# Shifted operand addresses and an earlier place for one triangular inverse in a two-layer hybrid backbone kernel

## The chip, the cores and the metric

The kernel runs on one core of a Trainium2 chip. The metric is the device time of one execution in microseconds; lower is better. The kernel before takes 1970.32 us, the median of three runs from 1968.26 to 1972.65. The computation is in float32 throughout; where a dense product is meant, each operand is split into a high and a low part and three products (high x high, high x low, low x high) are summed.

## The reference, cut to what matters

Two layers act on 512 latent tokens and 256 context tokens of width 1024. Every sub-layer is an RMS norm, a modulation by vectors from the conditioning (adaLN), the work itself, another RMS norm, a gate and a residual sum.

```
layer 0: mixer = [spatial-gating MLP | bidirectional RWKV-7, 8 heads] behind one input projection (2944 columns),
         then one output product; then ConvFFN on latents and context
layer 1: mixer = bidirectional mLSTM, 4 heads, behind one input projection; output product;
         then ConvFFN on latents only

def conv_ffn(h, w_up, conv_w, conv_b, w_down, rows):
    a, b = jnp.split(h @ w_up, 2, axis=-1)          # w_up: 1024 x 5632
    a = dwconv1d(a, conv_w[1]) if rows is None else dwconv_grid(a, conv_w, rows)
    return (jax.nn.gelu(a + conv_b) * b) @ w_down   # w_down: 2816 x 1024

def rwkv7_scan(...):                                # one step per token, per head, per direction
    sa = einsum('bhvk,bhk->bhv', s, kk_t)
    s = s * w_t - sa[..., None] * b_t + v_t[..., None] * k_t
    y_t = einsum('bhvk,bhk->bhv', s, r_t)
```

The kernel does the RWKV scan in chunks of 64 tokens. Inside a chunk the steps depend on one another through a lower triangular matrix with ones on its diagonal, which has to be inverted for each chunk, head and direction.

## The kernel before, in words

**Dense products.** Weights are streamed from HBM by `load_w` (L118): a raw tile of 1024 columns, its high part written by ACT (L124) and its low part by DVE or POOL (L125). `proj_pass` (L259 to 269) multiplies one such tile, 8 blocks of 128 columns as weights in PE, by the 8 blocks of the transposed activations as the moving operand, 512 columns for the latents and 256 for the context: a pass is 24 matmuls into one PSUM bank, L266, L267 and L268 in turn. `down` (L1033) has it the other way: the activations' blocks are the weights in PE, and half of the streamed weight tile, 512 columns, is the moving operand, L1043 to L1045, with two PSUM banks per token tile. `proj_pass` serves layer 0's input projection, layer 1's and both FFNs' first products; `down` serves both output products and both FFNs' second products.

**Where tiles lie.** All on-chip tiles come from pools that are stacked in each partition's memory, some from the left end and some (`side="right"`) from the right. A tile's bytes are rounded up to a multiple of 32. What was allocated before decides a tile's address. In the built program the operands of dense products begin at these places beyond a multiple of 512 bytes: the projection of layer 0 has activations and weights at 480; the later stages have weight tiles at 352, normalized activations at 480, and the FFN's hidden activations (`hhi`, `hlo`) at 224. The last of these lie behind the tile `fpar`, which holds the FFN's convolution parameters, 220 columns.

**Layer 0's mixer** has two stages. In the projection stage the 8 heads are prepared as four pairs ("column tiles" `ct` 0 to 3): projections with a short convolution (`kr`, `v`), decay and key terms (`prep_e`), the chunks' triangular matrices (`prep_n`) and their inverse (`prep_t`, L580). Finished sets are stored to HBM. In the chain stage they are loaded back, and a recurrence walks over the chunks of two pairs at a time, one `lane` each, first pairs 0 and 1, then 2 and 3, in six blocks.

`prep_t` copies the matrix's diagonal blocks through a DVE transpose (L585), sets an identity on POOL (L587, L588), and then does 31 substitution steps, two DVE instructions each (L597, L599). It then transposes the result, copies it into the tile `TT` on ACT (L613, L614), makes the off-diagonal blocks by two rounds of small matmuls (L621, L630) with copies between (L624, L633), and stores `TT` to HBM (L636). All its work tiles have one buffer, which the next pair's inverse needs again.

**What sets the order.** The pieces are Python generators. `weave` takes from several of them in turn, by the share of each one's steps that has been emitted (a third number delays a generator's start). Each `prep_t` yields after every third substitution step, after the copies to `TT`, and four times in the matmuls: 15 times in all. The framework then plans each engine's queue: emission order is the priority, and a planner with modelled durations gives an engine that would be idle the next instruction that is ready, even if it was emitted later. On the chip every queue runs in that planned order. The inverses of the third and the fourth pair (`ct` 2 and 3) are `Ts[0]` and `Ts[1]`; they are emitted in blocks 0 and 1 of the chain stage. `inverse()` runs `Ts[1]` and then frees the inverses' memory, in which the loads for the next modulation vectors (`ada_job`) are placed.

Of the kernel before, what the change touches and what calls it, by code (L numbers as in the profile page):

```python
# [8 lines left out]
F32 = mybir.dt.float32  # L9
# [5 lines left out]
P = 128  # L15
# [36 lines left out]
PF = _Cols()  # L52
# [22 lines left out]
def _build(ctx, tc, xall, par, cst, ada_0, ada_w, ada_t, w_in, w_out, ffn_up, ffn_down, lora, wsT, a_bs, c_in, c_gate, c_out, mneg, parf, parm, out):  # L75
# [9 lines left out]
    def bank(name, role):  # L85

        turn[role] = turn.get(role, -1) + 1
        return pp.tile([P, 512], F32, tag=role[turn[role] % len(role)], name=name)
# [201 lines left out]
    def woven(*gens):  # L290

        live = [[g[0], 0, g[1], g[2] if len(g) > 2 else 0.0] for g in gens]
        while live:
            k = min(range(len(live)), key=lambda j: live[j][3] + (1 - live[j][3]) * (live[j][1] + 0.5) / live[j][2])
            try:
                next(live[k][0])
                live[k][1] += 1
            except StopIteration:
                live.pop(k)
            yield  # L300

    def weave(*gens):
        for _ in woven(*gens):
            pass

    def part_of(g, n):
        for _ in range(n):
            next(g)
            yield

    def run(gen):
        for _ in gen:
            pass
# [16 lines left out]
    with ExitStack() as lx:  # L330
# [102 lines left out]
        prbank = lambda name: bank(name, "2435")  # L433
# [119 lines left out]
        def prep_n(ct):  # L553

            s = st[ct]
            RBv = s["RB"].rearrange("p (u a t) -> p u a t", a=2, t=64)
            LBv = s["LB"].rearrange("p (u a t) -> p u a t", a=2, t=64)
            NF = wkT.tile([P, 56, 32], F32, tag="NF", name=f"NF{ct}", bufs=2)
            G.memset(NF[:, 24:32], 0.0)
            G.memset(NF[:, 32:56], 0.0)  # L560
            for g8 in range(3):
                px, py = bank(f"nx{ct}{g8}", "23"), bank(f"ny{ct}{g8}", "45")
                for k in range(8):
                    u = g8 * 8 + k
                    mm(px[0:64, k * 64:k * 64 + 64], LBv[0:64, u, u // 12, :], RBv[0:64, u, 0, :], start=True, stop=True)
                    mm(py[64:128, k * 64:k * 64 + 64], LBv[64:128, u, u // 12, :], RBv[64:128, u, 0, :], start=True, stop=True)
                us = slice(g8 * 8, g8 * 8 + 8)
                for (pp, b0, e) in ((px, 0, A), (py, 64, A)):
                    p3 = pp.rearrange("p (u t) -> p u t", t=64)
                    cpy = e.copy if e is A else e.tensor_copy  # L570
                    off = slice(32 + g8 * 8, 40 + g8 * 8)
                    cpy(NF[b0:b0 + 32, us], p3[b0:b0 + 32, :, 0:32])
                    cpy(NF[b0 + 32:b0 + 64, us], p3[b0 + 32:b0 + 64, :, 32:64])
                    cpy(NF[b0 + 32:b0 + 64, off], p3[b0:b0 + 32, :, 32:64])
                yield
            for k in ("RB", "LB"):
                nc.sync.dma_start(set_part(ct, k), s[k])
            s["NF"] = NF
# [270 lines left out]
        def kr(ct):  # L849
            st[ct] = {}  # L850
            for c0, tag in ((12, "kT"), (8, "rT")):
                st[ct][tag] = conv_tile(c0 + ct, wkP, tag, f"{tag}{ct}", 2)
                yield
# [5 lines left out]
        def chained(*gens):  # L859
            for g in gens:  # L860
                yield from g

        def start_prep(ct):
            PLt = keep.tile([P, 24], F32, name=f"PL{ct}")
            st[ct]["PL"] = PLt
            for k, n in SET:
                if k not in ("vT", "TT"):
                    st[ct][k] = wkS.tile([P, n], F32, tag=k, name=f"{k}{ct}")
            return prep_e(ct, st[ct]["kT"], st[ct]["rT"])
# [13 lines left out]
                yield  # L883

        NA = (4, 6, 6)
        run(kr(0))
        weave((start_prep(0), 8), (chained(v(0), kr(1), part(0)), 3 + 0))
        run(prep_n(0))
        for ct in range(3):
            n = NA[ct]  # L890
            weave(*([(prep_t(ct, prbank), 13, 0.0)] if ct < 2 else []), (chained(start_prep(ct + 1), prep_n(ct + 1)), 9 + 3, 0.0),
                  (chained(v(ct + 1), *([kr(ct + 2)] if ct < 2 else []), part(n)), 3 + n, 0.0))
        run(SG)
        ex.close()
        hx.close()
        rx.close()
        sx.close()
        Ts = [prep_t(ct, lambda name: bank(name, "7")) for ct in (2, 3)]
        fin = lx.enter_context(tc.tile_pool(name="fin0", bufs=1))
        ch = lx.enter_context(tc.tile_pool(name="chain0", bufs=1))  # L900
        ys = [[fin.tile([P, 2, w], F32, name=f"y{n}{w}") for w in (TC, TL)] for n in ("01", "23")]
# [50 lines left out]
        def inverse():  # L952
            yield from Ts[1]
            tx.close()
            late["p"] = lx.enter_context(tc.tile_pool(name="late0", bufs=1))
            nc.scalar.dma_start(lwg, lora[:, 1024:1536])
# [16 lines left out]
        for b, (k, g) in enumerate(blocks):  # L973
            n = (22, 20, 22 - 10 * k)[g]
            todo = [(part_of(C[k], n) if g < 2 or k else C[k], n)]
            if b < 5:
                kk_, gg_ = blocks[b + 1]
                todo.append((preps(pairs[kk_], gg_), 10))
            if b == 0:
                todo.append((Ts[0], 13))  # L980
            elif b == 1:
                todo.append((inverse(), 13))
            elif b < 5:
                todo.append((part_of(ada, (5, 6, 5)[b - 2]), (5, 6, 5)[b - 2]))
            if b == 3:
                for ct in range(2):
                    load_bv(ct)
                todo.append((finish((0, 1), ys[0], ("01", "01"), "ctx"), 8))
            elif b == 4:
                todo.append((finish((0, 1), ys[0], ("01", "01"), "lat"), 8))  # L990
            elif b == 5:
                todo.append((finish((2, 3), ys[1], ("01", "01"), "ctx"), 8))
            weave(*todo)
            if g < 2:
                run(part_of(C[k], 4))
            if b == 1:
                ada = ada_job([1, 2], late["p"], 2, 2048)
            if b == 2:
                C.append(chains(pairs[1], ys[1]))
            if b == 4:  # L1000
                run(ada)
                gate_rows(0, 0, "7")
                scale_vec(0, 1)
                load_bv(2)
                load_bv(3)
# [53 lines left out]
    def ffn(l, xt, hT, ctx_too, after, final=None, beneath=None):  # L1059

        with ExitStack() as fx:
            hidp = fx.enter_context(tc.tile_pool(name=f"fhid{l}", bufs=1))
            hid = [hidp.tile([P, NH, w], F32, tag=f"hid{g}", name=f"hid{l}{g}") for g, w in ((0, TL), (1, TC))[:2 if ctx_too else 1]]
            fpar = hidp.tile([P, PF.n], F32, name=f"fpar{l}")
            nc.scalar.dma_start(fpar, parf[l])
            sp = fx.enter_context(tc.tile_pool(name=f"fs{l}", bufs=1))
            fill = beneath(sp) if beneath else None
# [71 lines left out]


    strm.sub, strm.hi, strm.lo = nc.vector, 3, 3
    xp = ctx.enter_context(tc.tile_pool(name="x", bufs=1))
    H = {tg: ctx.enter_context(tc.tile_pool(name=f"H{tg}", bufs=1, side="right")) for tg in ("lat", "ctx")}
    xcx = ExitStack()
# [464 lines left out]
```

## Time and profile before

| what | value |
|---|---|
| median of three runs | 1970.32 us (1968.26 to 1972.65) |
| the profiled execution: device time, span | 1975.72 us, 1973.8 us |
| PE busy, DVE busy | 1854.0 us (94%), 1334.4 us (68%) |
| ACT busy, POOL busy | 800.1 us (41%), 306.9 us (16%) |
| granted PE clock, mean | 0.965 |
| HBM read, written | 199.31 MB, 26.39 MB |

The stages lie in the span about so: projection stage up to 377 us, chain stage to 625, output product to 700, FFN of layer 0 to 1270, mixer of layer 1 to 1540, output product to 1590, FFN of layer 1 to the end. Matmuls are pipelined: a matmul's own duration in the profile is longer than the time after which the next one starts, so the pace of a stream of them is read from their starts, or from their count in a stretch of time. Times in a single row are microseconds from the span's start, and line numbers are those of the kernel before.

### The profile page before, as it was taken

What the parts mean: (1) busy time and instruction counts of PE and PEld (TensorE: products, weight loads), DVE (VectorE), ACT (ScalarE), POOL (GpSimd) and SP (SyncE); (2) the same over time, 40 slices, a digit from 0 to 9 for tenths busy, and PEclk for the clock granted to TensorE, in tenths of its full rate; (3) what the DMA queues carried; (4) which work ended last, traced back from release to release, by engine and by line L of the source; (5) the groups of instructions that cost most, each with busy time, mean ns of one, the idle gap of its engine ahead of it and who ended that gap; (6) DMA issues with size and microseconds to landing.
All of it is one profiled execution on the core that took longest, in us unless ns stands there. A gap on an engine that the chain in (4) does not pass through costs nothing.

```text
span 1973.8 us, 31872 instructions
## 1 busy us (share of the span) xinstructions
PE 1854.0 (94%) x12411; PEld 1508.3 (76%) x12411; DVE 1334.4 (68%) x2669; ACT 800.1 (41%) x1429; POOL 306.9 (16%) x429
## 2 busy tenths in 40 slices
PE   6998789698898999999999998999999989999998
PEld 4777677587666888888888886778888768888886
DVE  4379675757345589999994337667777688777534
ACT  4364645534335442222222226475554353323222
POOL 2222222311000222223330002100110020000001
PEclk9999889788899999999999999999999999999999
DMA  7133121643764524444432224431111312222222
GB/s 292 54 123 123 57 103 55 182 123 83 204 184 138 182 99 160 150 160 165 161 134 76 97 96 160 151 92 44 33 43 44 139 56 96 96 96 96 88 94 86
DMA packets 102887, 227.77 MB, mean 115 GB/s; under 512 B 28224, under 2 KB 44048, under 8 KB 99664
## 3 DMA queue, kind: packets, MB, share of 16 engines
q1 hardware_dynamic: 100976, 222.26, 33.4%
q10 hardware_dynamic: 1760, 3.47, 0.5%
q8 instruction: 98, 1.61, 0.3%
q14 instruction: 53, 0.43, 0.1%
HBM read 199.31 MB, written 26.39 MB: 114 GB/s over the span
## 4 chain that ended last, share of the span: by engine, by line
PE 58%; DVE 2%; POOL 1%; ACT 1%; issue 1%; DMA 0%; DVEq 0%; SPq 0%; ACTq 0%; POOLq 0%
PE of L1044 5%; PE of L1043 5%; PE of L1045 5%; PE pl_fb L268 4%; PE pl_fb L266 4%; PE pl_fb L267 4%; PE pl_fa L267 4%; PE pl_fa L268 4%; PE pl_fa L266 4%; PE pd L1453 1%; PE pe L1430 1%; PE kv L1386 1%; PE pc_fa L267 1%; PE pc_fa L266 1%; PE pc_fb L266 1%; PE pc_fb L268 1%
## 5 line engine op out<-in xcount | busy, mean ns | idle before, releaser
L1091 DVE SCALAR_TENSOR_TENSOR cv<-pl_fa,fpar,cv 128x441 f32<-128x441 f32 (+2 forms) x352 | 243.1, 691 | 16.5 <-ACT cv L1080 11.3
L1045 PE MATMUL of<-hi_fd,hlo 128*128 128x512 f32 x440 | 173.4, 396 | 3.0 <-DVE hlo L1115 3.0
L1044 PE MATMUL of<-lo_fd,hhi 128*128 128x512 f32 x440 | 174.6, 397 | 1.4 <-DVE lo_fd L125 1.4
L1043 PE MATMUL of<-hi_fd,hhi 128*128 128x512 f32 x440 | 173.7, 397 | 0.0
L201 DVE SCALAR_TENSOR_TENSOR aj<-am,srb 128x512 f32<-128x512 f32 x224 | 163.3, 729 | 10.0 <-DMA am<-in_ada_t_dram 5.6
L1115 DVE TENSOR_TENSOR hlo<-hid,hhi 128x512 fp32r<-128x512 f32 (+1 forms) x66 | 39.2, 601 | 133.9 <-ACT hhi L1114 133.7
L1114 ACT ACTIVATE hhi<-hid 128x512 fp32r<-128x512 f32 (+1 forms) x66 | 36.7, 559 | 177.2 <-PE of L1044 173.5
L1045 PEld LDWEIGHTS of<-hi_fd,hlo 128*128 128x128 f32 x440 | 83.2, 189 | 22.6 <-DVE hlo L1115 3.4
L1044 PEld LDWEIGHTS of<-lo_fd,hhi 128*128 128x128 f32 x440 | 83.3, 189 | 21.5 <-DVE lo_fd L125 2.3
L125 DVE TENSOR_TENSOR lo_fd<-raw_fd,hi_fd 128x1024 fp32r<-128x1024 f32 x66 | 80.8, 1224 | 26.0 <-ACT hi_fd L124 25.8
L1043 PEld LDWEIGHTS of<-hi_fd,hhi 128*128 128x128 f32 x440 | 83.1, 189 | 19.8 <-ACT hi_fd L124 0.5
L222 POOL TENSOR_SCALAR rstd_p_f<-sq_f,sq_f 128x1 f32<-128x1 f32 x10 | 6.9, 689 | 569.6 <-ACT jk_f L1022 569.6
L124 ACT ACTIVATE hi_fd<-raw_fd 128x1024 fp32r<-128x1024 f32 x66 | 69.2, 1049 | 28.7 <-DMA raw_fd<-in_ffn_down_dram 12.2
L124 ACT ACTIVATE hi_fa<-raw_fa 128x1024 fp32r<-128x1024 f32 x44 | 46.4, 1054 | 79.0 <-PE pl_fb L267 64.4
L124 ACT ACTIVATE hi_fb<-raw_fb 128x1024 fp32r<-128x1024 f32 x44 | 46.7, 1061 | 69.6 <-PE pc_fa L267 38.5
L125 POOL TENSOR_TENSOR lo_fb<-raw_fb,hi_fb 128x1024 fp32r<-128x1024 f32 x22 | 59.4, 2699 | 88.8 <-ACT hi_fb L124 88.8
L125 POOL TENSOR_TENSOR lo_win<-raw_win,hi_win 128x1024 fp32r<-128x1024 f32 x23 | 57.5, 2503 | 90.9 <-ACT hi_win L124 90.0
L1093 ACT ACTIVATE cv<-cv 128x512 f32<-128x512 f32 x44 | 27.8, 632 | 106.7 <-DVE cv L1091 106.7
L267 PE MATMUL pl_fa<-h1f_latlo,hi_fa 128*128 128x512 f32 x176 | 69.6, 396 | 0.0
L266 PE MATMUL pl_fb<-h0f_lathi,hi_fb 128*128 128x512 f32 x176 | 69.6, 396 | 0.0
L268 PE MATMUL pl_fa<-h0f_lathi,lo_fa 128*128 128x512 f32 x176 | 69.6, 395 | 0.0
L267 PE MATMUL pl_fb<-h0f_latlo,hi_fb 128*128 128x512 f32 x176 | 69.5, 395 | 0.0
(695 smaller groups left out, 5507.4 us busy)
## 6 DMA issues: line engine op xcount, KB each, us to landing
raw_fd<-in_ffn_down_dram SPq DMA_DIRECT2D x66, 512.0 KB, 3.2
am<-in_ada_t_dram SPq DMA_DIRECT2D x112, 256.0 KB, 3.0
raw_fa<-in_ffn_up_dram SPq DMA_DIRECT2D x44, 512.0 KB, 3.3
raw_fb<-in_ffn_up_dram SPq DMA_DIRECT2D x44, 512.0 KB, 3.2
raw_win<-in_w_in_dram SPq DMA_DIRECT2D x23, 512.0 KB, 3.3
ada<-in_ada_dram SPq DMA_DIRECT2D x8, 1024.0 KB, 8.9
ada<-in_ada_w_dram SPq DMA_DIRECT2D x8, 1024.0 KB, 8.0
raw_cin<-in_c_in_dram SPq DMA_DIRECT2D x16, 512.0 KB, 3.4
```

Source lines behind the costliest of these rows:

```text
L124: nc.scalar.activation(hi[:, c], raw[:, c], AF.Copy)
L125: strm.sub.tensor_tensor(lo[:, c], raw[:, c], hi[:, c].bitcast(F32), ALU.subtract)
L201: V.scalar_tensor_tensor(place(f"aj{i}{h}{cnd}", "junk"), raw, 1.0, sb[cnd * 2 + h], ALU.mult, ALU.mult, accum_out=acc[:, cnd, h:h + 1])
L266: mm(p, wh[:, kt, :], hh[:, kt], start=(kt == 0), stop=False)
L267: mm(p, wh[:, kt, :], hl[:, kt], start=False, stop=False)
L268: mm(p, wl[:, kt, :], hh[:, kt], start=False, stop=(kt == KT - 1))
L1043: mm(o[i][hf], hi, w[0][:, c], start=f, stop=False)
L1044: mm(o[i][hf], hi, w[1][:, c], start=False, stop=False)
L1045: mm(o[i][hf], lo, w[0][:, c], start=False, stop=e)
L1091: V.scalar_tensor_tensor(dv, src[:, r0 + dy:r1 + dy, c0 + dx:c1 + dx], fw(ky * 3 + kx), dv, ALU.mult, ALU.add)
L1114: A.activation(hi, hid[cnd][:, k], AF.Copy)
L1115: V.tensor_tensor(lo, hid[cnd][:, k], hi.bitcast(F32), ALU.subtract)
```

## The change

Three edits. First, two pools that hold one unused tile each are opened between layer 0's mixer and everything behind it, 160 bytes a partition on the left and 480 on the right. Second, the tile `fpar` is allocated with 256 columns and used with its first 220. Third, the generators of the third and fourth pair's inverses are made earlier; seven yields of the third pair's (21 of the 31 substitution steps) are emitted in the last weave of the projection stage; block 0 of the chain stage emits the rest of it and six yields (18 steps) of the fourth pair's; block 1 emits the remaining nine.

```diff
         NA = (4, 6, 6)
+        Ts = [prep_t(ct, lambda name: bank(name, "7")) for ct in (2, 3)]
         run(kr(0))
...
         for ct in range(3):
             n = NA[ct]
-            weave(*([(prep_t(ct, prbank), 13, 0.0)] if ct < 2 else []), (chained(start_prep(ct + 1), prep_n(ct + 1)), 9 + 3, 0.0),
+            weave((prep_t(ct, prbank), 13, 0.0) if ct < 2 else (part_of(Ts[0], 7), 7, 0.2), (chained(start_prep(ct + 1), prep_n(ct + 1)), 9 + 3, 0.0),
                   (chained(v(ct + 1), *([kr(ct + 2)] if ct < 2 else []), part(n)), 3 + n, 0.0))
...
-        Ts = [prep_t(ct, lambda name: bank(name, "7")) for ct in (2, 3)]
...
             if b == 0:
-                todo.append((Ts[0], 13))
+                todo.append((chained(Ts[0], part_of(Ts[1], 6)), 14))
             elif b == 1:
-                todo.append((inverse(), 13))
+                todo.append((inverse(), 9))
...
-            fpar = hidp.tile([P, PF.n], F32, name=f"fpar{l}")
+            fpar = hidp.tile([P, 256], F32, name=f"fpar{l}")[:, :PF.n]
...
     strm.sub, strm.hi, strm.lo = nc.vector, 3, 3
+
+    ctx.enter_context(tc.tile_pool(name="gap", bufs=1)).tile([P, 40], F32, name="gap")
+    ctx.enter_context(tc.tile_pool(name="gapr", bufs=1, side="right")).tile([P, 120], F32, name="gapr")
```

## The prediction

> **What bounds the kernel now.** I read the page first, then the busy time by stretches, and then single matmuls in order of time. The page:
>
> ```profile
> PE 1854.0 (94%) x12411; PEld 1508.3 (76%) x12411; DVE 1334.4 (68%) x2669; ACT 800.1 (41%) x1429; POOL 306.9 (16%) x429
> ...
> PE 58%; DVE 2%; POOL 1%; ACT 1%; issue 1%; DMA 0%; DVEq 0%; SPq 0%; ACTq 0%; POOLq 0%
> ```
>
> PE is busy in 94% of the span, and of what the chain that ended last names nearly all is PE. A busy PE doesn't say at what pace it goes, so the second view counts instructions in stretches. The columns are the length, then busy time and count for each engine.
>
> ```profile
> 186.72:191.25 4.53, 4.53 (x21) 3.75 (x20) 4.32 (x10) 0.00 (x0) 0.93 (x1) 1.00 0.66 206
> ...
> 700.00:1072.00 372.00, 369.97 (x2102) 321.85 (x2101) 339.52 (x767) 103.10 (x152) 100.68 (x139) 1.00 0.42 144
> 1090.00:1180.00 90.00, 90.00 (x389) 72.98 (x388) 30.67 (x32) 25.32 (x32) 0.00 (x0) 1.00 0.27 95
> 1274.00:1540.00 266.00, 257.90 (x1421) 212.84 (x1422) 194.91 (x499) 145.12 (x297) 26.91 (x60) 0.98 0.17 50
> 1597.00:1843.00 246.00, 246.00 (x1059) 198.98 (x1058) 192.41 (x256) 81.25 (x98) 0.00 (x0) 1.00 0.26 93
> 1620.00:1820.00 200.00, 200.00 (x862) 162.15 (x861) 155.33 (x202) 62.43 (x75) 0.00 (x0) 1.00 0.27 95
> ```
>
> Inside the second FFN's first product (1620 to 1820) there are only 512-column matmuls. Their pitch, start to start, is 200 us / 861 loads of weights = 232.3 ns. In the first FFN's second product (1090 to 1180) it is 90 / 388 = 232.0. The granted clock is 1.00 in both, and DVE, ACT and DMA have room: DVE, the fullest, has 192 of 246 us and, in the first FFN, 340 of 372. So such stretches last as long as PE's stream, and a shorter pitch there shortens the kernel.
>
> The first row is a pass of 24 products in the projection stage, of the same shape and type, before any line that the change touches. Here it is one by one, with a pass of the first FFN behind it:
>
> ```profile
> 186.26 0.40 PE L267 MATMUL pl_vg<-h_latlo,hi_win 128*128 128x512 f32 x1
> 186.72 0.39 PE L266 MATMUL pl_vg<-h_lathi,hi_win 128*128 128x512 f32 x1
> ...
> 191.25 0.39 PE L268 MATMUL pl_vg<-h_lathi,lo_win 128*128 128x512 f32 x1
> ```
>
> ```profile
> 763.00 0.40 PE L266 MATMUL pl_fb<-h0f_lathi,hi_fb 128*128 128x512 f32 x1
> 763.24 0.39 PE L267 MATMUL pl_fb<-h0f_latlo,hi_fb 128*128 128x512 f32 x1
> 763.47 0.40 PE L268 MATMUL pl_fb<-h0f_lathi,lo_fb 128*128 128x512 f32 x1
> ...
> 768.60 0.28 PE L266 MATMUL pc_fb<-h0f_ctxhi,hi_fb 128*128 128x256 f32 x1
> ```
>
> From 186.72 to 191.25 there are 20 steps: 226.5 ns each. From 763.00 to 768.60 there are 24: 233.3 ns each, with 240 and 230 in turn. The projection pass keeps 226.5 although DVE is busy in 4.32 of its 4.53 us and DMA at 0.66, so other engines aren't what slows the FFN's stream. What differs is where the operands lie. By the built program's allocation, in bytes beyond a multiple of 512, the projection has moving operand and weights both at 480. The FFN's first product has 480 and 352, its second 352 and 224, the output products 352 and 480. Both unequal pairings that are shown run near 232, the equal one at 226.5.
>
> **The change part by part.** *Alignment.* A gap of 160 bytes goes ahead of every pool stacked from the left, and one of 480 ahead of those stacked from the right. So 352 becomes 512, and 480 on the right becomes 0. The parameter tile grows from 896 reserved bytes to 1024, so the second product's left operand goes from 224 to 224+160+128 = 512. All dense products after the first mixer then have both operands at 0. The gaps hold nothing and issue nothing. The parameter tile's DMA still carries 220 columns, one per FFN, off the path.
>
> No run here shows the pairing 0 and 0. The nearest row is the other equal pairing, 480 and 480. I take its pitch with the slower beginning of a pass (two steps of 230 from 186.26 to 186.72): 227.5. The gain is 232.3 - 227.5 = 4.8 ns. Bounds: 226.5 throughout (5.8), and 229 if each pass pays a longer beginning (3.3).
>
> How many: output product 8 x 6 x 2 x 3 = 288, first FFN 22 x 2 x 8 x 3 = 1056 and 22 x 6 x 2 x 3 = 792, second FFN 1056 and 528, second output product 192. Together 3912, all in stretches that PE fills. That is 18.8 us (12.9 to 22.7). The second mixer has another 408 (24 for the gates, 384 for its projection), between recurrences that wait for other engines. PE is busy in 257.9 of its 266 us, so some of it counts: 0 to 2.0 us, I take 60%, as if 245 more were on the path: 1.2 us, and 4157 in all.
>
> The 256-column products of the context go the other way.
>
> ```profile
> 191.83 0.28 PE L266 MATMUL pc_vg<-h_ctxhi,hi_win 128*128 128x256 f32 x1
> ...
> 194.23 0.28 PE L268 MATMUL pc_vg<-h_ctxhi,lo_win 128*128 128x256 f32 x1
> ...
> 760.16 0.28 PE L266 MATMUL pc_fa<-h0f_ctxhi,hi_fa 128*128 128x256 f32 x1
> ```
>
> Equal: 2.40 us / 20 = 120.0 ns. Unequal: 24 of them from 760.16 up to the pass at 763.00, 2.84 / 24 = 118.3. There are 1056 in the first FFN and 216 in the second mixer: 1272 x 1.7 = +2.2 us (0 to 2.2). Alignment sums to -18.8 - 1.2 + 2.2 = -17.8 us.
>
> A rule speaks against all of this. The pitch differs between pairings, 226.5 and 232.3. The Trainium skill ("TensorE: Matmul & The Clock Gate", Part 2) says that PE has two independent SBUF read ports, so that loading the next weights takes nothing from the running matmul, and its page "SBUF — State Buffer" (Specifications) gives lines of 16 bytes, of which 480, 352 and 224 are all multiples. By these two the pitch could not depend on the pairing, and the sum would be the inverse's part alone. The trace doesn't agree so far as the pairing is the cause.
>
> *The inverse.* The substitution of the third pair's triangular inverse (31 steps of two DVE instructions, after two memsets on POOL and a transpose on DVE) gets its first 21 steps emitted inside the last projection weave. The chain stage's first block then holds the rest and the first 18 steps of the fourth pair's, and the second block the remainder. But the planner fills idle engines ahead of the order of emission, and did so here:
>
> ```profile
> 312.72 0.95 POOL L587 MEMSET Ti<- 128x1024 f32 x1 [8.19 <-PE w L621]
> ...
> 320.65 0.21 DVE L597 TENSOR_TENSOR fs<-Ai,Ti 128x31 f32<-128x31 f32 x1
> ...
> 349.88 0.43 DVE L599 TENSOR_TENSOR Ti<-Ti,fs 128x256 f32<-128x256 f32 x1
> ...
> 437.97 1.96 DVE L585 STREAM_TRANSPOSE Ai<-NF 128x1024 f32<-128x1024 f32 x1
> ...
> 502.95 0.33 SPq L636 DMA_DIRECT2D setd<-TT  x1
> ...
> 510.40 2.56 SPq L943 DMA_DIRECT2D ttp<-setd  x4
> ```
>
> The third pair's substitution already starts at 320.65, while the projections run, and it can't start sooner: its memset waits for the second pair's products (312.72). So what this part says is already so in the kernel before. Emitted ahead of the fourth pair's preparation it could push that back on DVE by its late, long instructions (6 steps of 2 x 0.43, 5 us), and behind it wait the preparation's products on PE, its copies on ACT and the stores that the lanes' loads wait for; I take 0, since the early weave places put most steps behind the preparation's, and keep the 5 us in the worst case below. What really moves is the fourth pair: its transpose at 437.97 waits until the third pair's last products have freed the buffers, and its result leaves at 502.95, after which the fourth pair's lane loads it at 510.40. Emitted earlier in the first block, those products come sooner, and so does all behind them.
>
> ```profile
> 400.00:440.00 40.00, 39.90 (x763) 34.61 (x759) 19.11 (x56) 12.52 (x37) 4.74 (x11) 0.90 0.37 108
> 440.00:480.00 40.00, 37.25 (x785) 32.85 (x785) 35.81 (x121) 13.82 (x43) 8.46 (x17) 0.98 0.39 101
> 480.00:520.00 40.00, 33.99 (x534) 25.79 (x530) 15.04 (x38) 17.78 (x32) 0.80 (x2) 0.79 0.44 135
> ```
>
> DVE has 21 us free in 400 to 440, and PE falls to 34 of 40 us, at a clock of 0.79, in 480 to 520, where the fourth pair's tail and the change of lanes lie. Best case: with the tail out of that stretch PE is as full there as before it, at the full clock: 6.0 us of idle time and 0.21 x 34 = 7 us of clock, -13 us. Worst case: 18 steps of two instructions between 0.21 and 0.43 us, some 10 us in all, go ahead of the lanes' small copies on DVE in the first block, and the lanes' products wait for those; with the 5 us above, +15. PE's stream in 400 to 440 is full already, so products put there push others out; I take a third of the best case, -4. Moved with it on the queues: the two memsets on POOL (0.95 us for the large one), ahead of its state products, and on SP the store of the result, and the modulation loads that wait for the inverse's memory; both come earlier, into a DMA share of 0.37 to 0.44.
>
> *Sum.* -17.8 - 4 = -21.8 us on the profiled execution's 1975.7 (span 1973.8). That execution is 5.4 us above the median of the runs, 1970.3, to which I apply it: 1948.5.
>
> **The rivals.** *Addresses do nothing.* Then the projection's 226.5 is of its stage: two PSUM banks in turn, other weights. For: one stage alone is equal-paired. Against: the second FFN product changes bank every three matmuls and the first every 24, and both read 232. Time: 1970.3 - 4 = 1966. The skill's two-port rule would give this.
>
> *The overhead goes altogether.* 480 starts 32 bytes short of a boundary, 0 on it.
>
> ```profile
> 1327.07 1.72 PE qk L1380 x4
> ```
>
> Here plain fp32 takes 430 ns per 512 columns in each of its two entries; at twice that rate it would be 215. At 215 and, for 256 columns, 108, the gain is 17.3 x 4157 + 10.3 x 1272 = 85 us: 1881. Against: equal passes are steady at 226.5, and 120.0 for half the columns, an overhead of some 12 ns for either width, which looks like a fixed cost per matmul.
>
> *Same place, same time (slower).* With both streams starting on a boundary every product could pay the slow step of the FFN pass, 240 (763.00 to 763.24): 7.7 x 4157 = +32 us, 1998 with the inverse's part. For: equal pairing is slower at 256 columns. Against: it is faster at 512. It decides against the change from a pitch of 233.3 on (4 us / 4157 = 1.0 ns above now).
>
> *Only the inverse goes wrong*: alignment as forecast and +15 us: 1967.5.
>
> **How the numbers follow.** The forecast has 0.66 (its own range 1936 to 1960), no effect of addresses 0.14, the inverse's cost 0.08, the whole overhead gone 0.07, the collision 0.05. The range 1929 to 1969 holds nearly all of the first, most of the second and half of the third. A measurement here can tell 0.2%, about 4 us. Faster: 0.66 + 0.07 + 0.07 + 0.04 = 0.84. Same: half of the second and the third, 0.11. Slower: 0.05.
>
> **What would show it.** Right: stretches inside the second FFN at 226 to 229 ns a product, and context passes at 120; the fourth pair's transpose before 430 and its store before 490; the projection stage unchanged to 1% up to 360. Wrong: a pitch of 232 in the FFN (addresses do nothing), or 215 (overhead gone), or over 233; the lanes' load of the fourth pair no earlier than 510, or the first block longer by more than the second is shorter. A DVE that fills the first FFN's stretch (340 of then 363 us) would cap the gain there.

## The result, and the profile after

The changed kernel takes 1950.56 us (median of four runs, 1946.71 to 1954.37) against 1971.49 us of the kernel before beside it (1968.26 to 1974.81). The ratio is 0.9897, with a 95% interval of 0.9874 to 0.9920. That is 20 us less (16 to 25).

The profiled execution took 1946.71 us, with a span of 1944.9. The busy time by stretches, of the changed kernel. The columns are the length, then busy time and count of PE, of PE's weight loads, of DVE, ACT and POOL, then the granted clock, the DMA share and GB/s:

```profile
1600.00:1800.00 200.00, 200.00 (x884) 165.62 (x883) 157.78 (x207) 63.20 (x76) 0.00 (x0) 1.00 0.28 98
1074.00:1164.00 90.00, 90.00 (x399) 74.53 (x398) 31.10 (x33) 26.37 (x34) 0.00 (x0) 1.00 0.28 100
...
1253.40:1519.40 266.00, 256.34 (x1420) 211.56 (x1421) 194.81 (x496) 145.82 (x297) 27.14 (x60) 0.99 0.16 50
```

Inside the second FFN's first product the pitch is now 200 / 883 = 226.5 ns (232.3 before), inside the first FFN's second product 90 / 398 = 226.1 (232.0 before). The third row is the mixer of layer 1: 1421 loads in 266 us, and 1422 before. Nothing is gained there.

Single instructions of the changed kernel in order of time: a context pass and a latent pass of the first FFN, each by its first row.

```profile
747.76 0.28 PE L266 MATMUL pc_fa<-h0f_ctxhi,hi_fa 128*128 128x256 f32 x1
...
750.64 0.40 PE L266 MATMUL pl_fb<-h0f_lathi,hi_fb 128*128 128x512 f32 x1
...
756.10 0.28 PE L266 MATMUL pc_fb<-h0f_ctxhi,hi_fb 128*128 128x256 f32 x1
```

The context pass takes 2.88 us / 24 = 120.0 ns, the latent pass 5.46 / 24 = 227.5. The same view for the inverses:

```profile
313.52 0.21 DVE L597 TENSOR_TENSOR fs<-Ai,Ti 128x31 f32<-128x31 f32 x1
...
420.86 1.97 DVE L585 STREAM_TRANSPOSE Ai<-NF 128x1024 f32<-128x1024 f32 x1
...
485.89 0.33 SPq L636 DMA_DIRECT2D setd<-TT  x1
...
495.07 2.56 SPq L943 DMA_DIRECT2D ttp<-setd  x4
```

The fourth pair's transpose stands at 420.86 (437.97 before), its store at 485.89 (502.95), its lane's load at 495.07 (510.40). But the whole chain stage starts earlier in this profile. Its first product, and the first of the output product behind it, in the kernel before and in the changed one:

```profile
390.62 0.30 PE L691 MATMUL c<-W,AZ 128*64 128x64 f32 x2
...
627.23 0.47 PE L1043 MATMUL oo<-hi_wo,a_lathi 128*128 128x512 f32 x1 [1.03 <-ACT a_lathi L1160]
```

```profile
381.12 0.22 PE L691 MATMUL c<-W,AZ 128*64 128x64 f32 x1
...
616.26 0.77 PE L1043 MATMUL oo<-hi_wo,a_lathi 128*128 128x512 f32 x1 [1.35 <-ACT a_lathi L1163]
```

These two places cut the span in three. The 28.9 us between the two spans divide as 9.5 up to the chain stage, 1.5 in it (236.6 to 235.1) and 18.0 behind it (1346.6 to 1328.6). The medians are only 21 us apart, so some of this is not the change's. The table below, read the same way from all profiles, says which.

| kernel | operands differ by (bytes) | chain starts at | chain stage | behind it, to the end |
|---|---|---|---|---|
| before | 128 | 390.6 | 236.6 | 1346.6 |
| before again | 128 | 385.2 | 238.4 | 1348.3 |
| third pair's part alone | 128 | 383.7 | 234.8 | 1350.5 |
| inverse's edit alone | 128 | 382.5 | 234.8 | 1347.2 |
| inverse's edit, later in the block | 128 | 385.2 | 227.3 | 1349.0 |
| fourth pair's part alone | 128 | 384.6 | 227.2 | 1352.2 |
| differences of 64 and 32 | 64, 32 | 386.8 | 236.2 | 1339.9 |
| addresses alone, 0 and 0 | 0 | 384.0 | 237.1 | 1329.0 |
| addresses alone, 480 and 480 | 0 | 385.2 | 236.5 | 1329.3 |
| addresses alone, difference 256 | 256 | 390.1 | 236.3 | 1329.3 |
| the changed kernel | 0 | 381.1 | 235.1 | 1328.6 |
| addresses and fourth pair's part | 0 | 385.4 | 224.9 | 1329.5 |
| the same, context 64 bytes lower | 0, 64 | 380.7 | 228.3 | 1325.9 |

The last column follows the operands' difference: 1346.6 to 1352.2 where it is 128, 1328.6 to 1329.5 where it is 0 or 256. The chain stage follows the order of the inverses, to about 3.5 us: the two kernels at the bottom have the same order and differ by 3.4. The start of the chain stage follows neither: where the inverses' order in the projection stage is that of the kernel before, it goes from 380.7 to 390.6.

### The profile page after: what moved, and what is told of

Read it like the earlier page. It is cut to its first block, busy times and chain, and to the rows that moved or that the text cites. A ratio compares the mean times of both kernels' runs of the same rounds, so it can differ in the third digit from the quotient of the medians.

```text
span 1944.9 us, 31874 instructions
## 1 busy us (share of the span) xinstructions
PE 1825.8 (94%) x12411; PEld 1501.0 (77%) x12411; DVE 1332.6 (69%) x2669; ACT 800.8 (41%) x1429; POOL 305.7 (16%) x429
## 4 chain that ended last, share of the span: by engine, by line
PE 58%; DVE 2%; ACT 2%; POOL 1%; issue 1%; POOLq 0%; DVEq 0%; ACTq 0%
PE of L1044 5%; PE of L1045 5%; PE of L1043 5%; PE pl_fb L267 4%; PE pl_fb L268 4%; PE pl_fb L266 4%; PE pl_fa L267 4%; PE pl_fa L266 4%; PE pl_fa L268 4%; PE pd L1456 1%; PE pe L1433 1%; PE pc_fb L268 1%; PE pc_fa L268 1%; PE pc_fb L267 1%; PE pc_fa L267 1%; PE pc_fb L266 1%
## 5 line engine op out<-in xcount | busy, mean ns | idle before, releaser
L266 PE MATMUL pl_fa<-h0f_lathi,hi_fa 128*128 128x512 f32 x176 | 69.0, 392 | 0.0
L267 PE MATMUL pl_fa<-h0f_latlo,hi_fa 128*128 128x512 f32 x176 | 68.8, 391 | 0.0
```

The lines of the kernel that those rows point to most:

```text
L266: mm(p, wh[:, kt, :], hh[:, kt], start=(kt == 0), stop=False)
L267: mm(p, wh[:, kt, :], hl[:, kt], start=False, stop=False)
```

## The experiments

**The addresses alone.** The gaps and the wider parameter tile, with the inverses as before.

```diff
+    ctx.enter_context(tc.tile_pool(name="gap", bufs=1)).tile([P, 40], F32, name="gap")
+    ctx.enter_context(tc.tile_pool(name="gapr", bufs=1, side="right")).tile([P, 120], F32, name="gapr")
...
-            fpar = hidp.tile([P, PF.n], F32, name=f"fpar{l}")
+            fpar = hidp.tile([P, 256], F32, name=f"fpar{l}")[:, :PF.n]
```

> Only the first two edits (the gaps of 160 and 480 bytes and the wider parameter tile); the inverses are emitted as before. Theory A (the pitch hangs on the pairing of the two operands' addresses modulo 512 bytes; pairing 0 and 0): 512-column products inside the second FFN's first product at 226.5 to 228 ns, context products at 119.7 to 120.0, and the time 15 to 19 us under the kernel before, ratio 0.990 to 0.9925. Theory B (the gain of the changed kernel comes from the earlier inverse and its queues): pitch near 227 all the same would refute it; by it the time would be within 5 us of the kernel before. If the projection stage, which the edit doesn't touch, is as long as in the kernel before (landmark: the last start of the normalization's tail near 368 us), then the 8 us by which the changed kernel's profile was ahead there belong to the inverse's edit or to the difference between executions.

Measured: 1950.65 against 1972.04, ratio 0.9906 (0.9873 to 0.9938). The second FFN by stretches:

```profile
1605.00:1805.00 200.00, 200.00 (x884) 165.66 (x883) 157.94 (x207) 63.36 (x76) 0.00 (x0) 1.00 0.28 98
```

Again 226.5 ns. Theory A holds: nearly the whole gain of the change is the addresses'.

**The inverse's edit alone.** The third edit as in the changed kernel, without gaps and with the parameter tile as before.

```diff
+            weave((prep_t(ct, prbank), 13, 0.0) if ct < 2 else (part_of(Ts[0], 7), 7, 0.2), (chained(start_prep(ct + 1), prep_n(ct + 1)), 9 + 3, 0.0),
...
+                todo.append((chained(Ts[0], part_of(Ts[1], 6)), 14))
...
+                todo.append((inverse(), 9))
```

> Only the third edit (the third pair's inverse begun in the last projection weave, the fourth pair's begun in the chain stage's first block); no gaps, the parameter tile as before. The prediction's term: -4 us (-13 to +15). From the changed kernel's profile: the chain stage is 1.5 to 2 us shorter, so theory A gives -1 to -4 us, ratio 0.998 to 0.9995, with the pitch of the FFN at 232 as before and the projection stage unchanged. Rival C (the edit also shortens the projection stage, by the 8 us that the pair of profiles shows there): -9 to -11 us, ratio 0.9945 to 0.9955.

Measured: 1968.01 against 1972.04, ratio 0.9987 (0.9973 to 1.0000). The chain stage takes 234.8 us, and it starts at 382.5. The second number alone would speak for rival C, but the time doesn't.

**The kernel before, again,** for that number.

> The kernel before, unchanged, for the part of the profiles' difference that no edit explains. If the 8 to 9 us by which the projection stage differs between the two profiles is a difference between executions: the chain stage starts anywhere from 383 to 391 us and the rest, from there to the end, is within 3 us of the first profile (1583 us). If it belongs to the kernels: 390 to 391 us again.

The same two places as above, in this second profile of the kernel before:

```profile
385.18 0.36 PE L691 MATMUL c<-W,AZ 128*64 128x64 f32 x2
...
623.53 0.47 PE L1043 MATMUL oo<-hi_wo,a_lathi 128*128 128x512 f32 x1 [1.94 <-ACT a_lathi L1160]
```

The chain stage starts 5.4 us earlier than in the first profile of the same kernel. From there to the end it is 1586.7 us for 1583.2, a little more than the 3 us of difference that were expected. What varies shows in the granted clock of a stretch with the same PE work, from the first product into `pl_kT` to the last, in the kernel before and then in the changed one:

```profile
79.00:236.00 157.00, 143.25 (x1011) 115.49 (x1011) 112.24 (x175) 89.35 (x149) 43.52 (x32) 0.92 0.27 101
```

```profile
76.50:229.00 152.50, 139.26 (x1010) 112.80 (x1009) 111.45 (x174) 88.91 (x148) 43.34 (x32) 0.96 0.28 103
```

1011 and 1009 loads took 157.0 us at a clock of 0.92 and 152.5 at 0.96. So most of the 9.5 us, or all, can be a difference between executions. The runs with the third pair's part start the chain stage at 381.1 to 385.2, inside the range of those without it, 380.7 to 390.6. The means, 383.1 and 385.8, don't exclude a share of some 2 us, but the third pair's part alone, below, gains nothing in time.

**Equal, but no multiple of 512.** One gap of 128 bytes on the left and the wider parameter tile, so that all operands lie at 480.

```diff
+    ctx.enter_context(tc.tile_pool(name="gap", bufs=1)).tile([P, 32], F32, name="gap")
...
-            fpar = hidp.tile([P, PF.n], F32, name=f"fpar{l}")
+            fpar = hidp.tile([P, 256], F32, name=f"fpar{l}")[:, :PF.n]
```

> One gap of 128 bytes on the left, none on the right, and the wider parameter tile: every dense product after the first mixer then has both operands at 480 bytes past a multiple of 512, equal to one another and no multiple. The inverses as before. Theory A1 (equality of the two places counts): the same pitch as with 0 and 0, 226.5 to 228 ns, the same time as with the gaps of 160 and 480 to within 3 us. Theory A2 (whole multiples of 512 count): pitch 232 as before and the time within 4 us of the kernel before, or a gain of less than a third of that.

Measured: ratio 0.9903 (0.9883 to 0.9924), and 883 loads in 200 us of the second FFN, as with 0 and 0:

```profile
1606.00:1806.00 200.00, 200.00 (x884) 165.62 (x883) 157.73 (x206) 63.21 (x76) 0.00 (x0) 1.00 0.28 98
```

Whole multiples of 512 are not needed, so A2 falls.

**Multiples of 256, unequal by 256.** Gaps of 160 and 224 bytes, the parameter tile at 1280.

```diff
+    ctx.enter_context(tc.tile_pool(name="gap", bufs=1)).tile([P, 40], F32, name="gap")
+    ctx.enter_context(tc.tile_pool(name="gapr", bufs=1, side="right")).tile([P, 56], F32, name="gapr")
...
+            fpar = hidp.tile([P, 320], F32, name=f"fpar{l}")[:, :PF.n]
```

> Gaps of 160 bytes on the left and 224 on the right and the parameter tile at 1280 bytes: the FFN's first products then have their operands at 256 and 0, the second products at 0 and 256, the output products at 0 and 256: every one a difference of 256 bytes, and all multiples of 256. The inverses as before. Theory A1 (equal places modulo 512): pitch 231 to 234 as before, time within 4 us of the kernel before. Theory A3 (what counts is the place modulo 256, or modulo 64 or less): 226.5 to 228 and 15 to 19 us under.

Measured: ratio 0.9905 (0.9884 to 0.9927), 883 loads in 200 us once more:

```profile
1610.00:1810.00 200.00, 200.00 (x884) 165.66 (x883) 158.10 (x208) 63.97 (x76) 0.00 (x0) 1.00 0.28 97
```

A1 falls too: a difference of 256 is as good as none.

**Differences of 64 and 32.** Gaps of 160 and 416 bytes, the parameter tile at 1056.

```diff
+    ctx.enter_context(tc.tile_pool(name="gap", bufs=1)).tile([P, 40], F32, name="gap")
+    ctx.enter_context(tc.tile_pool(name="gapr", bufs=1, side="right")).tile([P, 104], F32, name="gapr")
...
+            fpar = hidp.tile([P, 264], F32, name=f"fpar{l}")[:, :PF.n]
```

> Gaps of 160 and 416 bytes and the parameter tile at 1056: the operands of the first products then differ by 64 bytes (64 and 0), of the output products by 64 the other way, of the second products by 32. The inverses as before. Theory A3a (places have to be equal modulo 256): pitch 230 to 234, within 4 us of the kernel before. Theory A3b (only a difference near 128 is slow): 226.5 to 228 and 15 to 19 us under the kernel before, ratio 0.9905 to 0.9925.

Measured: ratio 0.9968 (0.9949 to 0.9987). The second FFN's first product (64) and the first FFN's second product (32):

```profile
1612.00:1812.00 200.00, 200.00 (x875) 164.09 (x875) 158.12 (x206) 64.02 (x76) 0.00 (x0) 1.00 0.28 96
1081.00:1171.00 90.00, 90.00 (x388) 72.44 (x387) 30.78 (x33) 25.34 (x32) 0.00 (x0) 1.00 0.27 94
```

200 / 875 = 228.6 ns and 90 / 387 = 232.6. Neither A3a nor A3b: a difference of 64 costs 2 ns, one of 32 as much as 128.

**Passes by themselves, by place.** The kernel of passes.

```diff
+        for s in range(24):
...
+            mo = m // 4 + a * cols
+            wo = w // 4 + b * 128
+            mm(p, W[:, wo:wo + 128], M[:, mo:mo + cols], start=(s == 0), stop=(s == 23))
```

> This kernel leaves the whole computation out: it copies the latent input to the output and runs, back to back, passes of 24 matmuls of the kernel's dense type, each pass with its operands at chosen places past a multiple of 512 bytes (moving operand first, weights second), 512 or 256 columns wide, every pass twice. By the runs so far a difference of 0 or 256 between the two places costs 226.5 to 227 ns at 512 columns, and a difference of 128 costs 232. Theory A3 (only the difference modulo 256 counts): pairs with difference 0, 256, wherever both lie, at 226.5 to 227.5; 128 and 384 at 231 to 234 in either direction. Between them open: any difference of 64 or less could cost as much as 128 (A3a, equality modulo 256 is what counts), or nothing (A3b, only the half-way case is slow), or be graded. For 256 columns: 119.5 to 120.2 at difference 0 and 118 to 119.5 at 128.

Each row is one pass of 24, the first column its start, so that two starts give the pitch. `paab` has places 0 and 0, `paag` 32 and 0, `paai` 64 and 0, `paao` 256 and 0; the 256-column passes are `pabk` (0 and 0), `pabn` (64 and 0) and `pabp` (128 and 0).

```profile
21.22 5.60 PE L112 MATMUL paab<-M,W 128*128 128x512 f32 x24
26.66 5.60 PE L112 MATMUL paac<-M,W 128*128 128x512 f32 x24
...
48.54 5.77 PE L112 MATMUL paag<-M,W 128*128 128x512 f32 x24
54.14 5.76 PE L112 MATMUL paah<-M,W 128*128 128x512 f32 x24
...
59.73 5.67 PE L112 MATMUL paai<-M,W 128*128 128x512 f32 x24
65.24 5.77 PE L112 MATMUL paaj<-M,W 128*128 128x512 f32 x24
...
93.27 5.63 PE L112 MATMUL paao<-M,W 128*128 128x512 f32 x24
98.73 5.67 PE L112 MATMUL paap<-M,W 128*128 128x512 f32 x24
...
214.90 3.02 PE L112 MATMUL pabk<-M,W 128*128 128x256 f32 x24
217.76 3.02 PE L112 MATMUL pabl<-M,W 128*128 128x256 f32 x24
...
223.42 2.89 PE L112 MATMUL pabn<-M,W 128*128 128x256 f32 x24
226.15 3.04 PE L112 MATMUL pabo<-M,W 128*128 128x256 f32 x24
...
229.02 3.01 PE L112 MATMUL pabp<-M,W 128*128 128x256 f32 x24
231.87 2.91 PE L112 MATMUL pabq<-M,W 128*128 128x256 f32 x24
```

5.44 / 24 = 226.7 ns at 0, 5.60 / 24 = 233.3 at 32, 5.51 / 24 = 229.6 at 64, 5.46 / 24 = 227.5 at 256. With 256 columns it is 119.2 at 0, 113.8 at 64 and 118.8 at 128. All differences, as the mean of the last 15 steps of a pass, where the start of the pass is over (each pass ran twice, and nearly all pairs repeat to 1 ns; the 0 column is of both operands at 0):

| moving minus weights, mod 512 | 0 | 16 | 32 | 48 | 64 | 96 | 128 | 160 | 192 | 224 | 256 | 320 | 384 | 448 | 480 | 496 |
|---|---|---|---|---|---|---|---|---|---|---|---|---|---|---|---|---|
| 512 columns, ns | 226.7 | 232 | 233 | 230.1 and 233.5 | 228.9 | 233.3 | 232.4 to 233.7 | 234.4 | 233.4 | 233.3 | 226.7 to 227.3 | 228.9 | 232.1 to 232.9 | 233.3 | 233.4 | 233.4 |
| 256 columns, ns | 120.0 | 116.5 to 118.7 | 116.9 | not run | 113.3 | 120.2 | 118.7 | not run | 113.3 | not run | 120.0 | not run | 118.7 | not run | not run | not run |

As far as the pairs go (0 and 256, 64 and 320, 128 and 384, 192 and 448), the difference counts modulo 256, and its sign counts: with the moving operand 64 above the weights a product of 512 columns takes 228.9 ns, with 64 below (448) 233.3. With both at the same place, 0, 32, 64, 128, 256 and 480 give 226.7 to 227.3; both at 16 give 231.1. Whether the weights are new in each matmul, the same three times, or always the same makes no difference beyond 1.3 ns.

**The third pair's part alone.** Its first seven yields (21 substitution steps) in the last projection weave, as in the changed kernel; the fourth pair's inverse as before. In block 0:

```diff
             if b == 0:
-                todo.append((Ts[0], 13))
+                todo.append((Ts[0], 8))
```

> Of the inverse's edit only the third pair's part: seven steps of its substitution emitted in the last projection weave, the rest in the chain stage's first block; the fourth pair's whole inverse in the second block as before; no gaps. The prediction's reading (the planner had already begun the third pair's there): no effect, from the chain stage's start to the output product 236 to 237 us, as in the kernel before (236.6), time within 2 us of it. Rival: this part carries the gain, 234.8 to 235.2 as with the whole edit.

Measured: ratio 1.0001 (0.9984 to 1.0017). The substitution begins 70.0 us ahead of the chain stage, as in the kernel before (390.62 - 320.65 = 70.0). The chain stage is 234.8 us, the rival's number, but the time shows no gain.

**The fourth pair's part alone.** The third pair's inverse whole in block 0, the first six yields (18 steps) of the fourth's behind it.

```diff
             if b == 0:
-                todo.append((Ts[0], 13))
+                todo.append((chained(Ts[0], part_of(Ts[1], 6)), 21))
             elif b == 1:
-                todo.append((inverse(), 13))
+                todo.append((inverse(), 9))
```

> Of the inverse's edit only the fourth pair's part: its first six steps emitted in the chain stage's first block behind the third pair's, which is emitted there whole, as before; no gaps. The prediction's reading (what moves is the fourth pair): the fourth pair's transpose and its store about 7 us earlier against the start of the chain stage than in the kernel before (47.4 and 112.4 us behind it), from there to the output product 234.8 to 235.5 us (236.6 before), time 1 to 3 us under the kernel before. Rival: no change in these places, the gain comes with the third pair's part.

Measured: 1962.15 against 1970.41, ratio 0.9962 (0.9950 to 0.9973), more than expected. The fourth pair's transpose and store:

```profile
419.56 2.00 DVE L585 STREAM_TRANSPOSE Ai<-NF 128x1024 f32<-128x1024 f32 x1
...
479.70 0.99 SPq L636 DMA_DIRECT2D setd<-TT  x1
```

Behind the chain stage's start (384.56), the transpose is at 35.0 us (47.3 before, 39.7 in the changed kernel), the store at 95.1 (112.3 and 104.8). The chain stage takes 227.2. So the fourth pair is what moves, and the whole edit loses most of what its second half wins.

**The whole edit, later in the block.** As the inverse's edit alone, with one number more: a delay puts the inverses' steps in block 0 where they stand in the run above. Against that run only the place of the third pair's first seven yields differs.

```diff
-                todo.append((chained(Ts[0], part_of(Ts[1], 6)), 14))
+                todo.append((chained(Ts[0], part_of(Ts[1], 6)), 14, 0.333))
```

> The whole edit of the inverse without gaps, but in the chain stage's first block the inverses' steps start after a third of the block, which is where the same steps stand when the third pair's inverse is emitted whole there. It differs from the fourth pair's part alone only in where the third pair's first seven steps are emitted. Theory D (the third pair's steps in the projection stage cost nothing; the whole edit does worse than the fourth pair's part because the rest then comes earlier in the first block): from the chain stage's start to the output product 227 to 229 us and 6 to 9 us under the kernel before. Theory E (it is the emission in the projection stage that costs): 233 to 236 us and 1 to 4 us under.

Measured: 1963.49 against 1970.14, ratio 0.9955 (0.9937 to 0.9973), chain stage 227.3. Theory D holds. The steps in the projection stage cost nothing. What costs is the place in block 0 of what is left of the third pair's inverse, seven yields shorter. Its 192 products of 32 x 32 stand in two runs in the kernel before, 10 to 17 and 35 to 46 us behind the chain stage's start, and here, 10 to 14 and 25 to 33. In the changed kernel they are spread thin from 10 to 38. The whole chain stage, then its stretches from 20 to 50 and from 85 to 145 us, for the kernel before, the changed one and this one:

```profile
390.62:627.23 236.61, 216.78 (x3632) 166.48 (x3629) 127.84 (x382) 88.33 (x213) 21.23 (x48) 0.92 0.49 138
410.60:440.60 30.00, 29.91 (x565) 26.54 (x563) 16.59 (x48) 7.20 (x22) 3.53 (x8) 0.85 0.33 101
475.60:535.60 60.00, 50.25 (x819) 38.06 (x817) 24.32 (x72) 23.02 (x47) 2.62 (x7) 0.80 0.56 154
```

```profile
381.12:616.26 235.14, 216.20 (x3632) 165.75 (x3629) 126.92 (x382) 88.24 (x213) 21.54 (x48) 0.93 0.48 139
401.10:431.10 30.00, 29.48 (x426) 24.09 (x425) 14.68 (x43) 5.95 (x18) 4.19 (x8) 0.72 0.20 58
466.10:526.10 60.00, 54.47 (x1073) 43.80 (x1074) 26.45 (x82) 24.15 (x56) 4.35 (x11) 0.94 0.60 183
```

```profile
385.19:612.46 227.27, 205.51 (x3631) 158.08 (x3629) 127.12 (x382) 88.94 (x213) 21.44 (x48) 0.98 0.51 144
405.20:435.20 30.00, 28.11 (x631) 24.67 (x628) 21.84 (x69) 9.87 (x28) 5.42 (x11) 1.00 0.35 106
470.20:530.20 60.00, 55.47 (x1018) 43.01 (x1014) 25.88 (x79) 20.48 (x52) 3.64 (x9) 0.97 0.61 182
```

Both edits fill the second stretch, and its clock rises from 0.80 to 0.94 and 0.97. But the changed kernel pays for it in the first, where 426 products are done at 0.72 against 565 at 0.85 before and 631 at 1.00 here. Over the whole stage, with the same 3629 loads, the length goes with the clock: 236.6 us at 0.92, 235.1 at 0.93, 227.3 at 0.98, and 227.2 at 0.98 with the fourth pair's part alone. That the clock is the cause, and not a thin stream that both lowers the clock and takes longer, is argued, not shown.

**Addresses and the fourth pair's part together.** The diffs of the addresses alone and of the fourth pair's part alone, both.

> The changed kernel's gaps and parameter tile, and of the inverse's edit only the fourth pair's part (the third pair's inverse is emitted whole in the chain stage's first block, the first six steps of the fourth pair's behind it). If the two parts add, as the runs so far say (0.9906 for the addresses alone, 0.9962 for the fourth pair's part alone): ratio 0.987, 25 us under the kernel before and some 5 us under the changed kernel; from the chain stage's start to the output product 227 us. If they overlap: no better than the changed kernel (0.9897).

Measured: 1943.26 against 1970.14, ratio 0.9857 (0.9832 to 0.9883). The parts add (0.9906 x 0.9962 = 0.9868). By the medians the kernel is 7 us faster than the changed one; the two intervals just overlap (0.9874 to 0.9883).

**The context 64 bytes lower,** on top of it, with a gap that puts the next pool back.

```diff
+    ctx.enter_context(tc.tile_pool(name="gapc", bufs=1, side="right")).tile([P, 16], F32, name="gapc")
+    H["ctx"] = ctx.enter_context(tc.tile_pool(name="Hctx", bufs=1, side="right"))
...
+            ox.enter_context(tc.tile_pool(name="gapd", bufs=1, side="right")).tile([P, 112], F32, name="gapd")
             op = ox.enter_context(tc.tile_pool(name="act1", bufs=1, side="right"))
```

> As the run before this one, and the context's operand tiles 64 bytes lower (moving operand at 448, weights at 0), since 256-column passes in the run of passes took 113.3 ns at differences of 64 and 192 bytes against 120.0 at 0, and in the kernel with differences of 64 and 32 the context passes of the first FFN took 117.8. Theory (the difference modulo 256 decides, and the passes measured by themselves carry over): context passes at 113 to 118 ns, 1272 of them, so 2.5 to 8.5 us under the run before; against it stand 96 products of the context's output product, which then have their weights at 448 (229 to 233 ns for 227), 0.2 to 0.6 us. Rival: in the kernel the gain is lost in the stages' waits, no difference within 2 us.

Measured: 1938.77, ratio 0.9829 (0.9806 to 0.9853), the best of all. A context pass of the first FFN, by its first row and the next pass's:

```profile
741.13 0.28 PE L266 MATMUL pc_fa<-h0f_ctxhi,hi_fa 128*128 128x256 f32 x1
...
743.96 0.39 PE L266 MATMUL pl_fb<-h0f_lathi,hi_fb 128*128 128x512 f32 x1
```

2.83 / 24 = 117.9 ns for 120.0, which is 1272 x 2.1 = 2.7 us; behind the chain stage the profile is 3.6 us shorter. The gain is at the low end of what was expected: by themselves such passes took 113.3 (difference 192), and why that doesn't carry over whole stays open. The intervals of this run and the one before it overlap, so the step from the one to the other isn't settled by the times.

## Why the prediction was right, and where it was not

*Alignment, -17.8 us.* Right in cause, and in the size of its sum. Behind the chain stage the two profiles differ by 18.0 us: 0.9 in the output product, 4.1 and 3.9 in the first FFN's two products, 0.5 in the second mixer with its output product, 6.0 and 2.5 in the second FFN's. In the table the kernels with equal places lie 17 to 24 us under those with a difference of 128. The pitch of 227.5 was right for the first FFN's first product (227.5 in the pass shown). Over all its latent passes, waits left out, it is 228.4 for 233.2 before, just the 4.8 ns that were forecast. In the second FFN and in `down`'s stretches it is 226.1 to 226.5, the row's other bound, since no slow beginnings of passes appear there.

*The second mixer, -1.2.* It gave nothing: 1421 loads in 266 us for 1422. "PE is busy in 257.9 of its 266 us, so some of it counts" was the wrong reading. That a PE busy in a chain of small products is not one whose dense products set the pace is the likely reason; no run tests it.

*The context's +2.2.* The direction is right. But 118.3 was one pass; the mean of all context passes of the kernel before's first FFN is 118.9 against 119.7 after, so it costs 1 us. That these two misses cancel is luck.

*The inverse, -4.* By itself it gave 2.6 us (0 to 5.3). That the third pair's part is "already so in the kernel before" holds for its substitution: the first row is 67.6 us ahead of the chain stage after (381.12 - 313.52) and 70.0 before, and its part alone gives 1.0001. That "what really moves is the fourth pair" holds too. The landmarks were met (420.86 before 430, 485.89 before 490) by luck: 9.5 us of each is the earlier start of the chain stage in that execution and 7.6 are its own, with which alone they would stand at 430.4 and 495.4. The sign "the projection stage unchanged to 1% up to 360" was missed for the same reason: the chain stage starts 2.4% earlier in that profile. The step that failed is the one between: "Emitted earlier in the first block, those products come sooner, and so does all behind them", with a third of the best case for products that push others out. What went with the loss was not a crowded stream, as the prediction had it, but a thin one at a low clock: 426 products in 30 us, at 0.72. Put later in the same block, the edit gains 6.7 us by the medians and 9.3 in the chain stage, well towards the best case of 13. So -4 against -2.6 measured is no proof of the reasoning.

*The rivals.* Addresses do nothing: refuted, by the addresses alone. Same place, same time: refuted, 226.7 with both on a boundary. The overhead gone altogether: refuted; 13 ns are left for either width (last section), much as the prediction argued. The inverse's +15: it gained instead, though it shows where a loss would come from. That the equal pairing is needed, as the allocation of the kernel before suggested, was too narrow: a difference of 256 does as well.

The Trainium skill ("TensorE: Matmul & The Clock Gate", Part 2) says that PE's two SBUF read ports are independent, and that loading the next weights takes nothing from the running matmul. The passes by themselves disagree: nothing but the operands' places differs between 226.7 and 233.6 ns. What in the hardware ties the two places together, no run shows.

## What to carry to other kernels

Where PE's stream is the bound, put the moving operand and the weights at equal places modulo 256 bytes (for fp32 products of 512 columns through the split; both at a multiple of 32), and look at the pitch by counting loads in a stretch: a PE at 94% busy hid 2.5% of the pitch here, and 1% of the time. For 256 columns a difference of 64 or 192 is better still: 113.3 ns for 120.0 in passes by themselves, 117.9 in the kernel. When work is moved into a stretch of small products, look at the granted clock of that stretch before and after: by the medians this kernel lost there about two thirds of what the move had won.

## What the runs showed of the hardware

*What is left of the pitch.* In the changed kernel one context pass runs at half the clock:

```profile
1287.11:1291.81 4.70, 4.70 (x24) 4.70 (x24) 4.50 (x12) 3.63 (x4) 0.00 (x0) 0.50 0.18 53
```

From the second start to the last are 22 steps, 4.70 / 22 = 213.6 ns for 256 columns. Half of that is 106.8, and at the full clock such a pass takes 120.0: 13 ns more. For 512 columns it is 226.7 - 213.6 = 13 ns. The two widths at the full clock give the same without the slow pass: 256 columns more cost 226.7 - 120.0 = 106.7. So at half the clock nothing is added. What adds it at the full clock, and why a difference of 64 takes away half of it for 256 columns and not for 512, stays open.

*The clock falls while the profile has PE busy.* In the changed kernel's slow stretch, 3.4 us apart:

```profile
404.70:408.10 3.40, 3.40 (x53) 2.76 (x51) 1.46 (x6) 0.02 (x1) 0.00 (x0) 1.00 0.02 5
408.10:411.50 3.40, 3.40 (x38) 2.56 (x38) 0.22 (x2) 0.00 (x0) 0.40 (x1) 0.50 0.00 0
```

PE is busy throughout, by ends of matmuls that are modelled, and from 386 to 426 the view of its waits lists one, of 0.2 us. The clock's own records change in steps of 3.4 us; this period of half the clock lasts 17.1. The Trainium skill ("TensorE: Matmul & The Clock Gate", Part 1) has windows of that length, which agrees, and has the clock fall after an idle window, which this stretch doesn't show by its busy time. What stands in the first of the two rows is this:

```profile
406.22 0.29 PE L630 MATMUL t<-Wm,Tn 32*32 32x32 f32 x2
406.44 0.33 PE L725 MATMUL c<-W,LT 128*64 128x64 f32 x2
406.70 0.29 PE L630 MATMUL t<-Wm,Tn 32*32 32x32 f32 x2
406.93 0.33 PE L725 MATMUL c<-W,LT 128*64 128x64 f32 x2
```

The inverse's products of 32 x 32 take turns in pairs with the lanes' larger ones, 0.48 us for four: 192 columns in a time in which, at 106.7 ns for 256, 1150 fit. From 20 to 50 us behind the chain stage's start the trace of the changed kernel has 36 such changes, that of the edit put later 14, that of the kernel before 20. That these changes make PE look idle to whatever grants the clock is argued, not shown. The third pair's part alone speaks against it as the whole story: it has 30 of them, and a period of only 3.4 us.

A count of columns comes nearer than busy time. In the 3.4 us ahead of this fall the products that start stream 2176 columns, 0.27 of the 8160 that fit. In the chain stages of the table's 13 profiles, each fall comes behind 3.4 us with a share of 0.06 to 0.31. It is no rule: a few stretches of 0.22 to 0.31 kept the clock, and in the projection stage it also fell behind 0.5. No run varies the share alone.
